# Expert weights in 4 KB rows, routing by counting beside the attention's end, and a planner with new durations: one change to a fused two-block layer kernel

## The chip, the cores and the metric

One NeuronCore of one Trainium2 chip runs the whole program. The metric is device time in microseconds (us); each kernel is timed several times, and the median counts. One further execution was taken by the hardware profiler; all rows below come from it. TensorE is called PE, its weight loads PEld, VectorE DVE, ScalarE ACT, GpSimd POOL, and SP is the engine that issues the weight loads.

## The reference, cut to what matters

256 tokens of width 1024, float32 throughout. Four parts run one after the other: an attention layer ("a"), a mixture of experts ("m"), and two hybrid layers ("0", "1").

```python
# a: two attentions over the same normed tokens, gated and added
mix = sigmoid(g_a) * out_a + sigmoid(g_b) * out_b
x = x + mix @ w_out
# m: top-1 group of 4, then top-2 of the 4 experts in it; 16 experts of width 512
t = rms_norm(x, norm_ffn_g)
g_logits = t @ w_group + b_group;  e_logits = t @ w_router + b_router
...
hid = silu(t @ w_gate[e]) * (t @ w_up[e]);  y = sum_e combine[e] * (hid @ w_down[e])
x = x + y
# 0 and 1: HGRN2 recurrence (8 heads of 128) and sliding-window attention (16 heads of 64)
y = concat(o_h, o_a) @ w_out_2;  x = x + rms_norm(y, g_post)
```

## The kernel before

**Who sets the order.** The program is written as tasks (Python generators) that yield one instruction at a time. `Sched.run` picks the next instruction of each engine when the kernel is built, from a table of durations in `Sched.op`, from priorities (`P_EDGE` first, `P_IDLE` last) and from a model of when operands are ready. What runs on the chip is a fixed list for each engine. `keep_warm` puts in dummy products (tile `warm`, on a matrix of ones, 256 columns) where the planner believes that PE would stand idle; once they are in the list they run whether PE would have waited or not. All recorded instructions carry the line of one helper (L202 before, L216 after), so rows are told apart by their tiles.

**Loads.** `plan_*` lists all weight transfers in order. `loader` issues them on SP into buffers `raw` of 1 MB, as many as `K.raw_max` allows and slots are free. Weights of parts a, 0 and 1 are split into a rounded half and a remainder (tile `w`: one ACT copy and one DVE subtraction for each 128x1024) and multiplied in three fast products; expert weights are used as they are, in full float32, so a product runs as two records. For each expert there are four units of gate and up columns (2 x 512 KB each) and two of down (1 MB each). The rows of gate and up go to partitions as `(a p)`: row 128a+p to partition p, so a partition's two pieces in one transfer are 2 KB each; a row of down is 4 KB.

**The end of part a.** `out_proj` makes the products `acc<-w,mix` (96, with 48 for the first half of the columns of `mix`, then 24 for each tile t of 128 tokens, c halves in turn). After each of the four (t, c), `Edge.tile` adds to `x`, squares it on ACT, multiplies by the gain into `hn` and has PE transpose it (`bank<-cp,hn`) into `hT`.

**Routing.** `route` multiplies `hT` with the 20 router columns (`bank<-cp,hT`, 120 columns wide, of which 20 count), then finds group, first and second expert by a chain of small DVE operations (tile `route`); `places` counts each token's place on PE; `one_hot` builds `rows`; `group(0)` gathers the tokens of four experts (`acc<-rows,x`, `bank<-rows,x`) into `xt`, and the first expert product `bank<-raw,xt` follows. In an expert: 16 products `bank<-raw,xt` (gate and up), `hidden` (ACT and DVE on `route`, then two transposes `bank<-cp,route`), 8 products `bank<-raw,route` (down, one expert behind), `acc<-rows` (back to the tokens). At expert 12 there is a branch (`overflow`, not taken here) that stands in every engine's list.

**The hybrid layers.** Projections column by column (`acc<-hh,w`, `acc<-hl,w`), the last of them `z3`; its result goes through `c_z` (ACT exp, DVE min, ACT ln, ACT exp, DVE product, all on tile `hb`) before `heads(3)` multiplies `bank<-hb,V`; then `out_proj` over `og` (192 products).

Of the kernel before, what the change touches and what calls it, by code (L numbers as in the profile page):

```python
# [20 lines left out]
BIG = 1e30  # L21
# [7 lines left out]
def _pack():  # L29
# [24 lines left out]
    parts["rank"] = np.broadcast_to(BIG * (16 - np.arange(16)[None, :]), (128, 16))  # L54
# [78 lines left out]
class Sched:  # L133
# [29 lines left out]

    def op(self, eng, op, f, a, k):
# [152 lines left out]
    def run(self):  # L317
        while self.tasks:
# [45 lines left out]
            if op == "dma_start":  # L364
                self.clk[eng] = issued = start + (1040 if eng == "POOL" else 60)
# [32 lines left out]
WIDE = 6  # L398
# [6 lines left out]
def setup(ctx, tc, I):  # L405
# [29 lines left out]
    K.gT = K.const.tile([128, 8], F32, name="gT")  # L435
    K.lev = K.const.tile([128, 10, 64], mybir.dt.uint8, name="lev")
# [61 lines left out]
def loader(K, between):  # L498
# [5 lines left out]
    def load():  # L504
        yield ("if", lambda: K.go)
        for i, u in enumerate(K.plan):
# [4 lines left out]
            for src, c in u.pieces:  # L511
                yield nc.sync.dma_start(rv[:, :, c:c + src.shape[2]], src)
# [16 lines left out]
    for i, u in enumerate(K.plan):  # L529
        yield wait(loaded[i])  # L530
        if u.how == "whole":
            u.half = raws.pop(i)
            u.flag[0].done = True
            continue
# [769 lines left out]
def plan_moe(K):  # L1304
# [19 lines left out]
def moe(K, edge, done):  # L1324
# [3 lines left out]
    K.raw_max = MOE_RAW  # L1328
# [9 lines left out]
    class Rows:  # L1338


        def __init__(self, t):
# [5 lines left out]
            self.gm, self.gs, self.e1, self.e2, self.m, self.w = (take_(1) for _ in range(6))  # L1347
            self.og, self.ge = (take_(4) for _ in range(2))
            self.L = take_(20)
            self.ee, self.o1, self.o2, self.e3, self.mask, self.first = (take_(16) for _ in range(6))  # L1350
    R = [Rows(t) for t in range(2)]
    rank = K.c("rank")

    def first_max(r, val, m, out):

        n = val.shape[1]
        yield nc.vector.tensor_reduce(m, val, axis=AX.X, op=OP.max)
        yield nc.vector.scalar_tensor_tensor(out, val, m, rank[:, 0:n], op0=OP.is_equal, op1=OP.mult)
        yield nc.vector.tensor_reduce(r.m, out, axis=AX.X, op=OP.max)

    def route(t):

        r = R[t]
        yield wait(edge.flag[t][0], K.t_router)

        pw, b_ = yield from bank(K, [128, 20 * WIDE])
        pL = pw[:, 0:20]
        sl = slice(t * 128, (t + 1) * 128)
        for k in range(8):
            yield wait(edge.flag[t][k // 4])  # L1370
            yield nc.tensor.matmul(pw, K.hh[:, k, sl], K.wide[:, 20 * k:20 * (k + WIDE)], start=(k == 0), stop=(k == 7))
# [4 lines left out]
        yield nc.vector.tensor_scalar_mul(comb[:, t, 16:17], scale, -1.0)  # L1376
        K.tinies.release(i)
        yield from first_max(r, r.L[:, 0:4], r.gm, r.og)
        g4 = lambda a: a.rearrange("p (g e) -> p g e", e=4)
        yield nc.vector.scalar_tensor_tensor(g4(r.ee), r.og[:, :, None].to_broadcast([128, 4, 4]), r.m, g4(r.L[:, 4:20]),  # L1380
                                             op0=OP.subtract, op1=OP.add)
        yield nc.vector.tensor_scalar(r.ge, r.L[:, 0:4], r.gm, None, op0=OP.subtract)
        yield from first_max(r, r.ee, r.e1, r.first)
        yield nc.vector.tensor_scalar(r.e3, r.first, r.m, -BIG, op0=OP.is_equal, op1=OP.mult)
        yield nc.vector.tensor_scalar(r.o1, r.first, r.m, None, op0=OP.is_equal)
        yield nc.vector.tensor_tensor_reduce(r.e3, r.e3, r.ee, 1.0, -3e38, OP.add, OP.max, r.e2)
        yield nc.vector.scalar_tensor_tensor(r.first, r.e3, r.e2, rank, op0=OP.is_equal, op1=OP.mult)
        yield nc.vector.tensor_reduce(r.m, r.first, axis=AX.X, op=OP.max)
        yield nc.vector.scalar_tensor_tensor(r.mask, r.first, r.m, r.o1, op0=OP.is_equal, op1=OP.add)

    def weights(t):

        r = R[t]
        yield wait(t_mask[t])
        yield nc.scalar.activation(r.ge, r.ge, AF.Exp, accum_out=r.gs)
        yield nc.vector.tensor_sub(r.e2, r.e2, r.e1)
        yield nc.scalar.activation(r.e2, r.e2, AF.Exp)
        yield nc.vector.scalar_tensor_tensor(r.w, r.e2, 1.0, r.gs, op0=OP.add, op1=OP.mult)
        yield nc.vector.reciprocal(r.w, r.w)
        yield nc.vector.tensor_sub(r.o2, r.mask, r.o1)  # L1400
        yield nc.vector.scalar_tensor_tensor(r.o1, r.o2, r.e2, r.o1, op0=OP.mult, op1=OP.add)
        yield nc.vector.tensor_scalar_mul(comb[:, t, 0:16], r.o1, r.w)
# [24 lines left out]
    t_mask = [sp(route(t), P_EDGE) for t in range(2)]  # L1427
    t_pos = [sp(places(t), P_EDGE) for t in range(2)]
# [31 lines left out]
    def halves():  # L1460
# [3 lines left out]
        for t in range(2):  # L1464
            yield from split(K, xhl[0][0][:, t], xhl[1][0][:, t], K.x[:, t])
# [5 lines left out]
    def group(q):  # L1471
# [7 lines left out]
        def part(k):  # L1479
            early = q == 0 and k < 6  # L1480
            yield wait(t_one[0] if early else t_one, t_half if q else None)
            res = K.accs if early and k < 4 else K.banks
            pg, b_ = yield from (acc_tile if res is K.accs else bank)(K, [128, 4, CAP])
# [753 lines left out]
```

## Time and profile before

| | us |
|---|---|
| three timed runs: median (lowest to highest) | 995.18 (995.14 to 996.44) |
| the profiled execution, its own time | 995.24 |
| its span, first to last instruction | 993.5 |
| PE busy | 979.1 |
| DVE busy | 691.4 |
| ACT busy | 501.2 |

The span is 1.7 us shorter than the execution's own time. The share of the span in which an engine is busy tells which engine has no room left, and dummy products count as busy. DMA moved 210.34 MB.

### The profile page before, as it was taken

What the parts mean: (1) busy time and instruction counts of PE and PEld (TensorE: products, weight loads), DVE (VectorE), ACT (ScalarE), POOL (GpSimd) and SP (SyncE); (2) the same over time, 40 slices, a digit from 0 to 9 for tenths busy, and PEclk for the clock granted to TensorE, in tenths of its full rate; (3) what the DMA queues carried; (4) which work ended last, traced back from release to release, by engine and by line L of the source; (5) the groups of instructions that cost most, each with busy time, mean ns of one, the idle gap of its engine ahead of it and who ended that gap; (6) DMA issues with size and microseconds to landing.
All of it is one profiled execution on the core that took longest, in us unless ns stands there. A gap on an engine that the chain in (4) does not pass through costs nothing.

```text
span 993.5 us, 16750 instructions
## 1 busy us (share of the span) xinstructions
PE 979.1 (99%) x6385; PEld 750.9 (76%) x6385; DVE 691.4 (70%) x1746; ACT 501.2 (50%) x1070; POOL 28.9 (3%) x67
## 2 busy tenths in 40 slices
PE   9999999999999999999999999999999999999998
PEld 8877999888434343444588989898788898988887
DVE  5778977876355434533687799899858489899952
ACT  5556879842021111110354648687755265867841
POOL 0101000000000000000000000000100000000000
PEclk9999999999999999999999999999999999999999
DMA  8822683798799999999913415432947142443331
GB/s 304 307 69 88 209 304 109 266 343 301 267 393 373 395 392 396 393 386 343 365 36 92 149 58 171 128 125 72 334 129 252 43 128 76 138 129 127 127 107 43
DMA packets 122931, 210.34 MB, mean 212 GB/s; under 512 B 6142, under 2 KB 54512, under 8 KB 122848
## 3 DMA queue, kind: packets, MB, share of 16 engines
q1 hardware_dynamic: 121632, 206.01, 59.2%
q0 software_dynamic: 1216, 3.22, 1.0%
q8 instruction: 52, 0.85, 0.4%
q14 instruction: 31, 0.25, 0.1%
HBM read 208.17 MB, written 1.05 MB: 211 GB/s over the span
## 4 chain that ended last, share of the span: by engine, by line
PE 47%; DVE 6%; DMA 1%; issue 1%; POOL 0%; ACT 0%; DVEq 0%; POOLq 0%
PE acc L202 35%; PE bank L202 11%; DVE ha L202 2%; PE warm L202 1%; DVE ap L202 1%; DMA raw<-in_w_in_dram 1%; DVE hb L202 1%; DVE w L202 1%; DVE og L202 0%; POOL sq L202 0%; DVE tiny L202 0%; DVE x L202 0%; ACT za L202 0%; DVE hn L202 0%; ACT hb L202 0%
## 5 line engine op out<-in xcount | busy, mean ns | idle before, releaser
L202 DVE TENSOR_TENSOR w<-raw,w 128x1024 fp32r<-128x1024 f32 (+1 forms) x196 | 235.3, 1220 | 28.2 <-ACT w L202 27.1
L202 PE MATMUL acc<-hh,w 128*128 128x256 f32 x1280 | 244.2, 287 | 0.0
L202 ACT ACTIVATE w<-raw 128x1024 fp32r<-128x1024 f32 (+1 forms) x196 | 198.7, 1041 | 21.9 <-PE acc L202 11.1
L202 PEld LDWEIGHTS acc<-hh,w 128*128 128x128 f32 x1280 | 201.8, 191 | 3.7 <-issue 1.4
L202 PE MATMUL acc<-hl,w 128*128 128x256 f32 x640 | 184.0, 288 | 0.0
L202 PE MATMUL acc<-w,hh 128*128 128x512 f32 (+2 forms) x512 | 155.2, 380 | 0.0
L202 PEld LDWEIGHTS acc<-hl,w 128*128 128x128 f32 x640 | 122.3, 191 | 3.5 <-issue 1.7
L202 PE MATMUL bank<-raw,xt 128*64 128x512 f32 x512 | 119.4, 600 | 0.0
L202 PEld LDWEIGHTS acc<-w,hh 128*128 128x128 f32 x512 | 92.1, 188 | 16.9 <-issue 2.1
L202 PE MATMUL acc<-w,hl 128*128 128x512 f32 (+2 forms) x256 | 96.5, 377 | 0.0
L202 ACT ACTIVATE route<-bank,route 128x256 f32<-128x256 f32 x16 | 7.6, 474 | 166.2 <-PE bank L202 166.2
L202 PE MATMUL acc<-w,og 128*128 128x512 f32 x384 | 89.1, 391 | 0.0
L202 PEld LDWEIGHTS acc<-w,og 128*128 128x128 f32 x384 | 71.7, 188 | 14.7
L202 PEld LDWEIGHTS bank<-raw,xt 128*64 128x64 f32 x512 | 33.1, 136 | 55.0 <-issue 48.7
L202 DVE TENSOR_TENSOR ha<-ha 128x256 f32<-128x256 f32 (+5 forms) x216 | 71.6, 365 | 4.2 <-PE bank L202 4.0
L202 ACT ACTIVATE ap<-ap,tiny 128x256 f32<-128x256 f32 (+1 forms) x110 | 47.8, 448 | 27.3 <-DVE tiny L202 26.8
L202 PE MATMUL bank<-raw,route 128*64 128x512 f32 x256 | 60.4, 599 | 0.0
L202 PEld LDWEIGHTS warm<-ones 128*128 128x128 f32 x325 | 45.6, 201 | 15.4 <-issue 9.1
L202 PE MATMUL warm<-ones 128*128 128x256 f32 x325 | 54.5, 309 | 2.7 <-ACT ones L424 2.4
L202 PEld LDWEIGHTS acc<-w,hl 128*128 128x128 f32 x256 | 48.3, 189 | 7.3
L202 DVE TENSOR_SCALAR route<-route 128x256 f32<-128x256 f32 (+2 forms) x24 | 6.2, 272 | 57.7 <-ACT route L202 57.6
L202 PEld LDWEIGHTS bank<-raw,route 128*64 128x64 f32 x256 | 16.8, 136 | 28.8 <-issue 25.8
(276 smaller groups left out, 1350.5 us busy)
## 6 DMA issues: line engine op xcount, KB each, us to landing
raw<-in_w_in_dram SPq DMA_DIRECT2D x68, 1024.0 KB, 6.1
raw<-in_w_gate_dram SPq DMA_DIRECT2D x64, 512.0 KB, 10.1
raw<-in_w_up_dram SPq DMA_DIRECT2D x64, 512.0 KB, 10.6
raw<-in_w_down_dram SPq DMA_DIRECT2D x32, 1024.0 KB, 11.9
raw<-in_w_out_dram SPq DMA_DIRECT2D x20, 1024.0 KB, 5.2
raw<-in_cmp_k_w_dram SPq DMA_DIRECT2D x2, 1024.0 KB, 5.8
raw<-in_cmp_v_w_dram SPq DMA_DIRECT2D x2, 1024.0 KB, 5.6
raw<-in_w_fox_up_dram SPq DMA_DIRECT2D x2, 1024.0 KB, 12.2
```

Of the source, the lines that this page charges most:

```text
L202: go = lambda: f(*a, **k)
```

## The change

- **Loads.** Gate and up rows go to partitions as `(p a)`: partition p holds rows 8p to 8p+7, so the two rows of one transfer are one run of 4 KB. `x`, `gT` and the gather read every eighth column (`k::8`) to match.
- **Routing.** The transposes take `x` itself, before the square and without the gain, which is folded into the router columns once (`gw`, one more small load on POOL). The router product is 20 columns wide. Ranks are found by comparing all pairs and counting. `moe` is started while part a still runs, so that tile 0's routing can stand among the last products of `w_out`.
- **The planner's table.** Transfers cost by run length (`_transfer`), a fast product costs 13.5 instead of 3 above its columns, an issue on SP 400 instead of 60. This moves instructions on all engines, in all parts.

```diff
         if op == "dma_start":
-            cost = int(np.prod(aps[0].shape)) * 4 / 360.0 + (1 if eng == "SP" else 20)
+            cost = self._transfer(aps)
...
-                cost = max(n * (1 if n >= 256 else 4) / 2.4, 107.0) + 3
+                cost = max(n * (1 if n >= 256 else 4) / 2.4, 107.0) + 13.5
...
-            wr = [I[nm][0, e].rearrange("(a p) c -> p a c", p=128)[:, 2 * u:2 * u + 2] for nm in ("w_gate", "w_up")]
-            K.plan.append(Unit("gu", [(wr[0], 0), (wr[1], 512)], 2, 1024, "whole"))
+            wr = [I[nm][0, e].rearrange("(p a) c -> p a c", a=8)[:, 2 * u:2 * u + 2] for nm in ("w_gate", "w_up")]
+            K.plan.append(Unit("gu", [(wr[0], 0), (wr[1], 1024)], 2, 1024, "pair"))
...
-        pw, b_ = yield from bank(K, [128, 20 * WIDE])
-        pL = pw[:, 0:20]
+        pL, b_ = yield from bank(K, [128, 20])
...
-            yield nc.tensor.matmul(pw, K.hh[:, k, sl], K.wide[:, 20 * k:20 * (k + WIDE)], start=(k == 0), stop=(k == 7))
+            yield nc.tensor.matmul(pL, K.hh[:, k, sl], K.w20[:, k], start=(k == 0), stop=(k == 7))
...
+        v = r.L.rearrange("p (g e) -> p g e", e=4)
+        yield nc.vector.tensor_tensor(r.less, v[:, :, None, :].to_broadcast([128, 5, 4, 4]),
+                                      v[:, :, :, None].to_broadcast([128, 5, 4, 4]), op=OP.is_gt)
+        for j in range(1, 4):
+            yield nc.vector.tensor_tensor(r.less[:, :, j, 0:j], v[:, :, 0:j], v[:, :, j:j + 1].to_broadcast([128, 5, j]), op=OP.is_ge)
+        yield nc.vector.tensor_reduce(r.n.rearrange("p (g e) -> p g e", e=4), r.less, axis=AX.X, op=OP.add)
...
+        yield nc.vector.tensor_scalar(r.mask, r.mask, 2.0, None, op0=OP.is_lt)
...
-        yield from first_max(r, r.L[:, 0:4], r.gm, r.og)
...
-                    yield nc.tensor.matmul(pg, K.x[:, t, c], Pm[:, t].bitcast(F32), start=(t == 0), stop=(t == 1))
+                    yield nc.tensor.matmul(pg, K.x[:, t, k::8], Pm[:, t].bitcast(F32), start=(t == 0), stop=(t == 1))
...
+                if self.nxt == "m":
+
+                    ts.append(sp(transposed(K, t, c, K.x[:, t], self.flag[t][c]), P_EDGE))
                 yield nc.scalar.activation(h, xs, AF.Square, accum_out=sm[:, c:c + 1])
                 flags[1][c].done = True
-                yield nc.vector.tensor_mul(h, xs, K.gain[:, half(c)])
...
             if part == "a":
-                yield from layer1(K, edge, new.done)
+
+                before = sp(layer1(K, edge, new.done), P_MAIN)
...
-                yield from moe(K, edge, new.done)
+                yield from moe(K, edge, new.done, before)
```

Three places on PE show what moved. In these rows `xN` counts equal instructions in a run, here one for each product. First, the end of part a: the last products of `w_out` (`acc<-w,mix`), the transposes (`cp,hn` or `cp,x`), the router (`cp,hT`), the place counts (`route,cp`, `route,ones`), the gather (`rows,x`). Before:

```order
L202 MATMUL acc<-w,mix 128x512 x71
L202 MATMUL bank<-cp,hn 128x128 x4
L202 MATMUL acc<-w,mix 128x512 x14
L202 MATMUL bank<-cp,hn 128x128 x4
L202 MATMUL acc<-w,mix 128x512 x10
L202 MATMUL bank<-cp,hn 128x128 x4
L202 MATMUL acc<-w,mix 128x512
L202 MATMUL bank<-cp,hT 128x120 x10
L202 MATMUL bank<-cp,hn 128x128 x4
L202 MATMUL bank<-cp,hT 128x120 x6
L202 MATMUL warm<-ones 128x256 x14
L202 MATMUL bank<-route,cp 128x16
```

After, from tile 0's router on:

```order
L216 MATMUL bank<-cp,hT 128x20 x8
L216 MATMUL acc<-w,mix 128x512 x10
L216 MATMUL bank<-route,ones 128x16
L216 MATMUL bank<-cp,x 128x128 x4
L216 MATMUL bank<-route,cp 128x16
L216 MATMUL acc<-w,mix 128x512 x3
L216 MATMUL bank<-cp,hT 128x20 x4
L216 MATMUL acc<-w,mix 128x512 x5
L216 MATMUL acc<-rows,x 128x256 x2
L216 MATMUL bank<-cp,x 128x128 x4
L216 MATMUL acc<-rows,x 128x256 x2
L216 MATMUL bank<-cp,hT 128x20 x4
```

Tile 0's router and place count now stand ahead of the last 18 products of `w_out`, and part of its gather ahead of tile 1's last transposes. After these rows come two gather products, 2 dummies where 29 stood, tile 1's place count, two more gather products and the first expert product.

Second, the end of the experts, from the last part of expert 15's gate and up. Before:

```order
L202 MATMUL bank<-raw,xt 64x512 x4
L202 MATMUL warm<-ones 128x256 x6
L202 MATMUL bank<-raw,xt 64x512 x4
L202 MATMUL warm<-ones 128x256 x6
L202 MATMUL bank<-raw,route 64x512 x4
L202 MATMUL bank<-cp,route 128x128 x2
L202 MATMUL warm<-ones 128x256 x4
L202 MATMUL bank<-raw,route 64x512 x4
L202 MATMUL warm<-ones 128x256 x6
L202 MATMUL bank<-raw,route 64x512 x4
```

After:

```order
L216 MATMUL bank<-raw,xt 64x512 x10
L216 MATMUL bank<-raw,route 64x512 x8
L216 MATMUL warm<-ones 128x256 x29
L216 MATMUL bank<-cp,route 128x128 x2
L216 MATMUL warm<-ones 128x256
L216 MATMUL acc<-rows 128x512
L216 MATMUL bank<-raw,route 64x512 x2
```

Before, 13 runs of dummies (65 in all) stand between the products of experts 12 to 15; after, none until one run of 29 between down of expert 14 and the transposes of expert 15. Over the whole list dummies fall from 325 to 275.

Third, the end of a hybrid layer's projections (the same in both layers), from the last product of `z3`. Before:

```order
L202 MATMUL acc<-hh,w 128x256
L202 MATMUL bank<-ha 128x128 x2
L202 MATMUL warm<-ones 128x256
L202 MATMUL bank<-cp,ap 128x128
L202 MATMUL warm<-ones 128x256
L202 MATMUL bank<-cp,ap 128x128 x2
L202 MATMUL warm<-ones 128x256 x9
L202 MATMUL bank<-cp,ap 128x128 x3
L202 MATMUL acc<-w,og 128x512 x3
```

After:

```order
L216 MATMUL acc<-hh,w 128x256
L216 MATMUL warm<-ones 128x256 x42
L216 MATMUL bank<-hb,V 128x256
L216 MATMUL bank<-hb,V 128x128
L216 MATMUL bank<-hb,V 128x256
L216 MATMUL bank<-hb,V 128x128
L216 MATMUL acc<-w,og 128x512 x7
```

The attention products that stood here before (`ha`, `cp,ap`) are now earlier, and 42 dummies in one run follow `z3`, where 11 stood.

## Rows read from the trace of the kernel before

**Rows 1.** The page, part 1: busy time of each engine.

```profile
PE 979.1 (99%) x6385; PEld 750.9 (76%) x6385; DVE 691.4 (70%) x1746; ACT 501.2 (50%) x1070; POOL 28.9 (3%) x67
```

**Rows 2.** PE by stage: window, length, busy (records), granted clock, DMA share, GB/s.

```profile
16.70:236.20 219.50, 217.81 (x1434) 1.00 0.64 219
249.50:485.80 236.30, 236.00 (x1144) 1.00 1.00 372
500.20:743.40 243.20, 241.20 (x1762) 1.00 0.40 130
```

**Rows 3.** PE in order of time, two experts: start, duration, what.

```profile
392.00 4.51 PE L202 MATMUL bank<-raw,xt 128*64 128x512 f32 x20
...
404.65 4.51 PE L202 MATMUL bank<-raw,xt 128*64 128x512 f32 x20
```

**Rows 4.** SP in order of time: down's transfers of two experts that follow each other.

```profile
380.76 2.06 SPq L202 DMA_DIRECT2D raw<-in_w_down_dram  x2
...
396.67 1.92 SPq L202 DMA_DIRECT2D raw<-in_w_down_dram  x2
```

**Rows 5.** PE in order of time, the end of part a's attention.

```profile
194.95 2.18 PE L202 MATMUL warm<-ones 128*128 128x256 f32 x17
196.97 0.27 PE L202 MATMUL bank<-cp,np 128*128 128x128 f32 x1
197.69 1.05 PE L202 MATMUL bank<-cp,np 128*128 128x128 f32 x7 [0.45 <-ACT np L202]
```

**Rows 6.** PE from the end of w_out to the first expert product.

```profile
236.06 2.39 PE L202 MATMUL bank<-cp,hT 128*128 128x120 f32 x20
...
241.26 2.31 PE L202 MATMUL warm<-ones 128*128 128x256 f32 x14
...
249.50 1.94 PE L202 MATMUL bank<-raw,xt 128*64 128x512 f32 x8
251.37 1.99 PE L202 MATMUL acc<-rows,x 128*128 128x256 f32 x8
```

**Rows 7.** DVE at tile 1's routing: its chain's first step, and the step behind it.

```profile
242.99 0.23 DVE L202 SCALAR_TENSOR_TENSOR route<-bank,tiny,b 128x20 f32<-128x20 f32 x1
...
245.98 0.17 DVE L202 SCALAR_TENSOR_TENSOR route<-bank,route 128x16 f32<-128x16 f32 x1
```

**Rows 8.** Weight loads of the gather: count, shortest, median, longest ns.

```profile
L202 PEld LDWEIGHTS acc<-rows,x x16: 186/190/192, 247.1 to 252.8; 128*128 128x128 f32 x16
```

**Rows 9.** Dummies alone in the experts' end: window, length, PE busy, PEld busy, clock, DMA.

```profile
439.50:480.70 41.20, 11.40 (x65) 8.73 (x65) 1.00 0.96 354
```

**Rows 10.** PE at expert 15's hidden values.

```profile
474.07 1.06 PE L202 MATMUL warm<-ones 128*128 128x256 f32 x6
475.06 1.94 PE L202 MATMUL bank<-raw,route 128*64 128x512 f32 x8
477.07 0.41 PE L202 MATMUL bank<-cp,route 128*128 128x128 f32 x2
```

**Rows 11.** DMA as gate and up come, then down: all engines by window; last GB/s.

```profile
366.00:371.00 5.00, 5.00 (x27) 2.46 (x27) 0.49 (x2) 0.00 (x0) 0.00 (x0) 1.00 1.06 388
372.00:377.00 5.00, 5.00 (x26) 1.55 (x24) 3.24 (x7) 1.22 (x3) 0.00 (x0) 1.00 1.03 407
```

**Rows 12.** PE in the first hybrid layer, from z3's last product to w_out.

```profile
690.68 0.28 PE L202 MATMUL acc<-hh,w 128*128 128x256 f32 x1
691.21 0.68 PE L202 MATMUL bank<-ha 128*128 128x128 f32 x4 [0.25 <-DVE tiny L202]
...
692.96 2.10 PE L202 MATMUL warm<-ones 128*128 128x256 f32 x9
...
695.19 0.95 PE L202 MATMUL acc<-w,og 128*128 128x512 f32 x3
```

**Rows 13.** ACT at the same place: a split's copies.

```profile
687.93 1.99 ACT L202 ACTIVATE w<-raw 128x1024 fp32r<-128x1024 f32 x2
```

**Rows 14.** The page, part 6: w_out's transfers, count, size, median us to landing.

```profile
raw<-in_w_out_dram SPq DMA_DIRECT2D x20, 1024.0 KB, 5.2
```

More of the change, by code (lines that the diff above doesn't have):

```diff
@@ L162, in _region, with _transfer, run @@
         return p, p + n, f * b, e * b
+    @staticmethod
+    def _transfer(aps):
+        def run(x):
+            dims, n = [d for d in x.ap if d[1] > 1], 1
+            if x.space is not None and str(x.space) != "DRAM":
+                dims = [d for d in x.ap[1:] if d[1] > 1]
+            for step, m in reversed(dims):
+                if step != n:
+                    break
+                n *= m
+            return n
+        n = min(run(x) for x in aps[:2])
+        return int(np.prod(aps[0].shape)) / n / 16 * (8 + 0.0371 * 4 * n)
     def op(self, eng, op, f, a, k):
@@ L364, in run @@
             if op == "dma_start":
-                self.clk[eng] = issued = start + (1040 if eng == "POOL" else 60)
+                self.clk[eng] = issued = start + (1040 if eng == "POOL" else 400)
                 self.dma = end = max(self.dma, issued + 1040) + cost
@@ L1321, with moe @@
 MOE_RAW, MOE_END = 19, 11
-def moe(K, edge, done):
+def moe(K, edge, done, before):
     nc, I, sch = K.nc, K.I, K.S
@@ L1327, in moe, with more_raws @@
     ident = K.c("ident")
-    K.raw_max = MOE_RAW
+    def more_raws():
+        yield wait(before)
+        K.raw_max = MOE_RAW
+    t_raws = sp(more_raws(), P_EDGE)
     tr, s_r = yield from big(K, [128, 2048], "route")
@@ L1346, in take_ @@
                 return tr[:, o[0] - n:o[0]]
[L1347 to L1350, printed above, removed]
-    R = [Rows(t) for t in range(2)]
[L1352 to L1359, printed above, removed]
+            self.gm, self.gs, self.e1, self.es, self.w = (take_(1) for _ in range(5))
+            self.ge = take_(4)
+            self.L, self.n = (take_(20) for _ in range(2))
+            self.ee, self.mask = (take_(16) for _ in range(2))
+            self.less = take_(80).rearrange("p (g i j) -> p g i j", g=5, i=4)
+    R = [Rows(t) for t in range(2)]
     def route(t):
@@ L1425, in most @@
         K.banks.release(b_)
-    t_mask = [sp(route(t), P_EDGE) for t in range(2)]
-    t_pos = [sp(places(t), P_EDGE) for t in range(2)]
+    t_mask = [sp(route(t), P_EDGE if t else P_EVAC) for t in range(2)]
+    t_pos = [sp(places(t), P_EDGE if t else P_EVAC) for t in range(2)]
     t_w = [sp(weights(t), P_EVAC) for t in range(2)]
@@ L1464, in halves @@
         for t in range(2):
[L1465 removed]
+            yield from split(K, *(a[0][:, t].rearrange("p (k d) -> p k d", k=8) for a in xhl), K.x[:, t].rearrange("p (d k) -> p k d", k=8))
     def both(a, b):
@@ L1482, in part @@
             res = K.accs if early and k < 4 else K.banks
+            if res is K.banks and q == 0:
+                yield wait(edge.flag[1])
             pg, b_ = yield from (acc_tile if res is K.accs else bank)(K, [128, 4, CAP])
@@ L1501, in group @@
         if q == 0:
+            yield ("if", lambda: len(edge.tasks) == 2)
             yield wait(t_mask, edge.tasks)
+            yield wait(t_raws)
             K.slots.release(K.s_hh, edge.room[1])
@@ L2146, in sums @@
                     return
+                if self.nxt == "m":
+                    ts.append(sp(transposed(K, t, c, K.x[:, t], self.flag[t][c]), P_EDGE))
                 yield nc.scalar.activation(h, xs, AF.Square, accum_out=sm[:, c:c + 1])
                 flags[1][c].done = True
-                yield nc.vector.tensor_mul(h, xs, K.gain[:, half(c)])
-                if self.nxt == "m":
-                    yield from transposed(K, t, c, hn, self.flag[t][c])
+                if self.nxt != "m":
+                    yield nc.vector.tensor_mul(h, xs, K.gain[:, half(c)])
             r = None
@@ L2160, in tile @@
                 yield wait(ts)
-            ts = [sp(sums(c, r), P_EDGE) for c in range(2)]
+            ts = []
+            for c in range(2):
+                ts.append(sp(sums(c, r), P_EDGE))
             if self.nxt is not None:
@@ L2190, in main @@
         edge.first()
+        before = None
         for i, part in enumerate(parts):
```

58 lines of the change are left out of this document (31 added, 27 removed).

## The prediction

> **What bounds the kernel now.** I read the busy shares first. PE is busy 979.1 of 993.5 us, and no other engine comes near it [rows 1]. Next I read PE by stage: it stands idle 1.7 us of 219.5 in the attention part, 0.3 of 236.3 in the experts and 2.0 of 243.2 in the first hybrid layer, at a granted clock of 1.00 throughout [rows 2]. The second hybrid layer runs the same list. So nothing gets shorter unless PE has less in its list, or stands less. The list holds 325 dummy products, though, and those count as busy. Seventeen of them take from 194.95 to 196.97, so one takes 2.02 / 17 = 0.12 us [rows 5].
>
> The loads look like a second bound in the experts' stage, where DMA's share is 1.00 [rows 2]. They are not one yet. Two experts that follow each other start 404.65 - 392.00 = 12.65 us apart on PE [rows 3], while down's transfers are issued 396.67 - 380.76 = 15.9 us apart [rows 4]. PE eats faster than the loads come, and lives on the buffers that were full when it began. It never ran out: expert 15's own products stand back to back with dummies between them, and I see no product that starts late. So a faster load by itself buys no time here. It buys lead.
>
> My sum is therefore an account of PE: dummies that leave the list, stalls that go or come, and the dummies and stalls that are new.
>
> **The attention part.** Before, a run of 17 dummies, 2 more and a stall of 0.45 us stand before the last attention products [rows 5]: 2.0 + 0.2 + 0.45 = 2.7 us. After, the list has none there, since the up-projection of the other attention fills the place; 14 dummies at the start become 7 (-0.8). That is -3.5 at best. A planner that places operations closer to their operands may bring small stalls back; the stage had 1.7 us of them. I take -2.5; bounds -4 and +1.
>
> **The edge and the routing.** Before, PE leaves `w_out` at 236.0 and begins the first expert product at 249.50, 13.5 us later, with a run of 14 dummies and one of 15 between [rows 6]. Tile 1's chain on DVE starts with its logits at 242.99 and takes 2.99 us [rows 7]; tile 0's chain, of the same length, ran ahead of it on DVE in that gap. After, tile 0's chain lies beside products of `w_out`. That is not free: its router and place products now stand among them. A router product took 2.39 / 10 = 0.24 us [rows 6]; twelve of them, two place counts and some 0.5 us of waiting for copies move the end of `w_out` 3.7 us later. From that end I count tile 1's path: add to x and signal 0.9, transposes 0.4, copy 0.9, four router products 0.9, logits 0.3, seven counting steps 1.7 (the seventeen small operations of the old chain took 0.18 each, from 242.99 to 245.98; dependent ones take more, and I take 0.24), place count and its two signals 0.5, place 0.2, one-hot 0.4, small operations left on DVE, gather and scaling of the first `xt` 2.4. That makes 8.6. The first expert product comes at 3.7 + 8.6 = 12.3 us instead of 13.5, which is -1.2. By then 8 instead of 4 gather products are done, at 1.99 / 4 = 0.5 us each [rows 6], another -2.0.
>
> One thing speaks against it. The gather reads every eighth column of x as its stationary operand. Its weight loads now take 190 ns [rows 8] and hide under records 0.25 us apart. No row shows a load with that step. If it doubled, 32 records would take 0.13 us more each: +4.2. If it costs nothing, 0. I take +0.5, near nothing, because the present load leaves 0.06 us of cover. [...] Together the edge gives -2.7; bounds -5 and +2.
>
> **The experts.** The steady part does not change: same products, and the loads stay ahead. I check the lead, since PE gets earlier. Gate and up came at 388 GB/s, down in 4 KB rows at 407 [rows 11]. At 407, the 4.19 MB of an expert's gate and up take 10.3 instead of 10.8 us, some 0.5 us less, 5 us over the ten experts for which the loads are the slower side. That is more than PE gains on them before the tail. If the rate did not rise, the loads would still start as much earlier as PE frees their buffers.
>
> The tail holds the largest term. Thirteen runs of dummies there are busy for 11.4 us [rows 9], less 0.09 us by which each run's last overlaps the next product: 10.2 us. After, they are gone, but one run of 29 stands between down of expert 14 and the transposes of expert 15: 29 x 0.12 = 3.5 us, whatever PE would wait. Is it shorter than the wait? Before, gate and up end at 474.07 and the transposes begin at 477.07 [rows 10], so the hidden values take 3.0 us. In the changed ACT list two weight copies stand between exp and ln, 1.0 us each [rows 13]. That makes about 5.0, and down of expert 14 covers 3.6 of it (two of the runs of rows 10). So the dummies end last. The copy of the transposed values out of PSUM stands behind two more weight copies on ACT, about 1 us. The tail gives -10.2 + 3.5 + 1.0 = -5.7; bounds -8 and -1. The next edge loses 9 dummies of 79, at most -1.1; its chain on DVE sets its end, so I take -0.5.
>
> **The hybrid layers.** Here the change costs. Before, from the end of `z3`'s last product (690.96) to the first product of `w_out` (695.19) 4.2 us pass, in which 1.1 us are real products (one `ha` product and six transposes): a hole of 3.1 [rows 12]. After, the real products stand earlier and 42 dummies fill the place: 42 x 0.12 = 5.0 us that PE must run. The work that covered the wait is used up elsewhere, so the layer pays 5.0 - 3.1 = 1.9 more. The chain behind it (ACT exp, two copies of 1.0, ln, one copy, exp, then DVE) adds to about 6.3; if that held PE, it would be 3.2. Its result is not what `hb,V` multiplies, so I take 2.3 for each layer, +4.6 for both; bounds 0 (the products moved forward fill other stalls) and +12.
>
> **The rest.** One more small load on POOL and one DVE product of 160 elements lie in the first part of a, far ahead of the routing that needs them. If they were late, tile 0's router would wait, and the products of `w_out` behind it. Splitting x with a step is off PE's path.
>
> **The sum.** -2.5 - 2.7 - 5.7 - 0.5 + 4.6 = -6.8. From the profiled execution's 995.24 that is 988.4; its time stands 0.06 above the median of the timed runs, so nothing is to be corrected. I forecast 988.5; its own range is 985 to 992.
>
> **The rivals.**
> - **Slower: the hole in the hybrid layers.** If the ln of `c_z` waits for a weight copy whose load has not landed, each layer's hole becomes 6.3 plus a load's 5.2 [rows 14], and the two layers cost 2 x (11.5 - 3.1) = 16.8 instead of 4.6: 1000.6. It decides once a hole exceeds 3.1 + 5.7 = 8.8 us. For it: the copies stand in front of ln in ACT's list, and a list cannot be changed at run time. Against: before, copies at this place ran back to back [rows 13]. Chance 0.14.
> - **The loads become the bound in the tail.** PE comes 5 us earlier and loses its dummies there; if gate and up gain no rate, experts 14 and 15 wait for their buffers and the tail's 5.7 is given back: 994. Against: 407 over 388 GB/s is in the trace [rows 11]. Chance 0.11.
> - **The strided weight loads cost in full:** +3.7 on the sum, 992. [...] Chance 0.10.
> - **The hybrid layers cost nothing,** since the planner's better durations also take out the 2.0 us of stalls in each: 988.4 - 4.6 = 984. For it: every stall that it removes is PE time. Against: 42 dummies are in the list. Chance 0.15.
>
> **How the numbers follow.** The forecast has 0.50. I widen the range to 980 and 998, which takes in 984, 992, 994 and nearly half of the slower case. What a measurement of this kernel tells from no change is about 0.2%, 2 us: faster means under 993.2, slower over 997.2. Faster: 0.50 + 0.15 + 0.07 of the strided case, and little of the loads' case, 0.73. Same: the rest of these two, 0.12. Slower: 0.15.
>
> **What would show it.** In the changed profile, PE should start the first expert product about 4 us earlier (near 246) and the last of down 10 or more us earlier (near 475). The gap after `z3` should last 5 to 6 us, filled with dummies. Gate and up should come at about 407 GB/s, with no wait of PE for them. I would be wrong if stalls of under a microsecond appear all over the hybrid layers, which the present lists, planned with too short products, happened to cover; if the clock falls where dummies left; or if the hole at expert 15 lasts much longer than its 29 dummies.

## The result, and the profile after

The changed kernel takes 1005.65 us (median of four runs, 1004.63 to 1006.59); the kernel before, beside it on the same chip, 995.81 (995.14 to 996.48). The ratio is 1.0097, with a 95% interval of 1.0082 to 1.0112. It is about 1% slower; I had forecast 988.5.

I read where the time went from the first product of each stage on PE, in the timeline of both profiles. The table gives the lengths between these firsts in us: `start` up to the first projection product, `attention` up to the first `acc<-no,w`, `edge` up to the first `bank<-raw,xt`, `experts` up to the first `acc<-w,hh` of the first hybrid layer, each hybrid layer up to the end of its last `acc<-w,og`. The other columns are kernels that are explained below (E1: 13.5 for a fast product alone; E4: transfer costs alone; E5: loads alone; E6: routing alone; E7: routing and transfer costs).

| | before | after | E1 | E4 | E5 | E6 | E7 |
|---|---|---|---|---|---|---|---|
| start | 16.7 | 17.7 | 16.6 | 16.1 | 16.6 | 16.9 | 17.3 |
| attention | 184.6 | 186.0 | 184.7 | 184.5 | 184.8 | 185.4 | 185.8 |
| edge | 48.2 | 46.6 | 48.0 | 48.2 | 48.6 | 46.5 | 46.5 |
| experts | 250.7 | 249.8 | 252.1 | 246.1 | 255.2 | 252.8 | 246.3 |
| first hybrid layer | 243.2 | 248.3 | 248.2 | 243.1 | 243.1 | 243.2 | 243.0 |
| second hybrid layer | 243.3 | 248.3 | 248.2 | 243.2 | 243.3 | 243.2 | 243.3 |

After against before: start +1.0, attention +1.4, edge -1.6, experts -0.9, hybrid layers +5.0 each. That is the +9.9 between the two spans.

The page's busy line of the changed kernel, which answers to [rows 1], and PE by stage, which answers to [rows 2] (window, length, busy, granted clock, DMA share, GB/s):

```profile
PE 975.9 (97%) x6335; PEld 748.5 (75%) x6335; DVE 701.4 (70%) x1755; ACT 496.7 (50%) x1054; POOL 23.2 (2%) x64
```

```profile
17.70:242.26 224.56, 220.98 (x1434) 0.99 0.63 217
250.31:486.26 235.95, 228.02 (x1100) 0.99 0.99 382
500.15:748.41 248.26, 246.06 (x1792) 1.00 0.35 118
```

PE is still the bound, but it now stands idle 7.9 us among the experts where it stood 0.3, and the clock is no longer at 1.00 throughout. In the hybrid layer it is busy 5 us longer with the same products and 31 more dummies.

The first 44.0 us of the first hybrid layer, up to the first `acc<-hh,w`, are as long after as before. The rest in two parts, the projections up to the end of `z3`'s last product and what stands behind it, before and after:

```profile
544.19:690.96 146.77, 145.75 (x1289) 1.00 0.37 116
690.96:743.42 52.46, 51.82 (x240) 1.00 0.66 231
```

```profile
544.14:696.90 152.76, 151.06 (x1309) 1.00 0.31 97
696.90:748.41 51.51, 51.40 (x253) 1.00 0.67 235
```

The part with the 42 dummies got 0.95 us shorter; the projections ahead of them got 6.0 longer. Products that moved ahead of `z3` (`ha` 0.44, `cp,ap` 0.69, `ap,kv` 1.24, by their time on PE before) are 2.4 us of that. For the other 3.6 PE in order of time shows shorter runs. The score products of two heads, before and then after:

```profile
672.65 0.93 PE L202 MATMUL bank<-kv,qaT 64*128 64x128 f32 x8
```

```profile
673.99 0.92 PE L216 MATMUL bank<-kv,qaT 64*128 64x128 f32 x4
...
675.63 0.92 PE L216 MATMUL bank<-kv,qaT 64*128 64x128 f32 x4
```

Eight records in one run take as long as four (0.93 and 0.92 us): two heads' products, each on 64 rows, run beside each other when they are neighbours in the list (their records start in pairs, 0.01 us apart). After, they stand apart, and the second head costs 0.85 us more. In the list before one pair of heads stands apart too. Over the layer PE is busy 9.0 us with score products before and 9.9 after, waits left out.

PE behind `z3`, which answers to [rows 12]:

```profile
696.62 0.28 PE L216 MATMUL acc<-hh,w 128*128 128x256 f32 x1
696.75 3.50 PE L216 MATMUL warm<-ones 128*128 128x256 f32 x28
699.72 2.20 PE L216 MATMUL warm<-ones 128*128 128x256 f32 x17
701.76 1.47 PE L216 MATMUL bank<-hb,V 128*128 128x256 f32 x8
702.99 1.87 PE L216 MATMUL acc<-w,og 128*128 128x512 f32 x7
```

(Three of the dummies stand in both rows, where two windows meet.) The tail of the experts on all engines but PEld, which answers to [rows 10]:

```profile
467.66 3.60 PE L216 MATMUL bank<-raw,route 128*64 128x512 f32 x16
...
470.54 2.36 DVE L216 TENSOR_TENSOR w<-raw,w 128x1024 fp32r<-128x1024 f32 x2 [0.19 <-ACT w L216]
...
471.19 3.74 PE L216 MATMUL warm<-ones 128*128 128x256 f32 x29
471.36 0.46 ACT L216 ACTIVATE route<-bank,route 128x256 f32<-128x256 f32 x1
472.16 2.01 ACT L216 ACTIVATE w<-raw 128x1024 fp32r<-128x1024 f32 x2 [0.34 <-DMA raw<-in_w_in_dram]
472.82 0.29 DVE L216 TENSOR_SCALAR route<-route 128x256 f32<-128x256 f32 x1
473.25 2.36 DVE L216 TENSOR_TENSOR w<-raw,w 128x1024 fp32r<-128x1024 f32 x2
474.07 0.85 ACT L216 ACTIVATE route<-route 128x256 f32<-128x256 f32 x2
...
475.97 2.36 DVE L216 TENSOR_TENSOR w<-raw,w 128x1024 fp32r<-128x1024 f32 x2
...
478.24 0.48 DVE L216 SCALAR_TENSOR_TENSOR route<-bank,route 128x256 f32<-128x256 f32 x1
...
478.87 0.41 PE L216 MATMUL bank<-cp,route 128*128 128x128 f32 x2 [3.94 <-DVE route L216]
```

Between the steps of expert 15's hidden values stand splits of the next layer's weights, copies on ACT and subtractions of 2.36 us a pair on DVE. The 29 dummies end at 474.9; PE waits on to 478.87.

PE's windows of 2 us around two of its longest waits, columns as above:

```profile
110.00:112.00 2.00, 0.53 (x3) 0.84 1.11 365
112.00:114.00 2.00, 2.00 (x11) 0.50 1.04 344
114.00:116.00 2.00, 2.00 (x17) 0.80 0.19 64
480.00:482.00 2.00, 2.00 (x6) 0.50 1.06 369
482.00:484.00 2.00, 2.00 (x7) 0.64 1.10 351
```

Behind the wait of 3.94 us, and behind one of 2.30 us for DVE's `tq` at 111.47, PE runs for some 3.4 us at a granted clock of 0.50 (an estimate from these windows). In the first dip a fast product of 256 columns takes 0.21 to 0.22 us (from 114.07 to 114.28 and from 112.57 to 112.79 on PE), against 0.12 at a clock of 1.00. So I count a window of 2 us at clock c as a loss of 2 x (1 - c), and estimate the first dip at 0.3 + 1.0 + 0.4 and the second at 1.0 + 0.7: 1.7 us each.

### The profile page after: what moved, and what is told of

It reads as the page before. It is cut to its first block, busy times and chain, and to the rows that moved or that the text cites. A ratio compares the mean times of both kernels' runs of the same rounds, so it can differ in the third digit from the quotient of the medians.

```text
span 1003.4 us, 16635 instructions
## 1 busy us (share of the span) xinstructions
PE 975.9 (97%) x6335; PEld 748.5 (75%) x6335; DVE 701.4 (70%) x1755; ACT 496.7 (50%) x1054; POOL 23.2 (2%) x64
## 3 DMA queue, kind: packets, MB, share of 16 engines
HBM read 208.16 MB, written 1.05 MB: 208 GB/s over the span
## 4 chain that ended last, share of the span: by engine, by line
PE 46%; DVE 8%; ACT 1%; issue 1%; DVEq 0%
PE acc L216 32%; PE bank L216 12%; DVE ha L216 3%; DVE w L216 2%; PE warm L216 1%; DVE ap L216 1%; ACT ha L216 1%; DVE hb L216 1%; DVE hn L216 0%; DVE rows L216 0%; DVE tiny L216 0%; DVE x L216 0%; DVE og L216 0%; DVE za L216 0%; ACT w L216 0%
## 5 line engine op out<-in xcount | busy, mean ns | idle before, releaser
L216 PE MATMUL acc<-hh,w 128*128 128x256 f32 x1280 | 247.4, 289 | 0.0
L216 PE MATMUL acc<-hl,w 128*128 128x256 f32 x640 | 184.8, 289 | 0.0
L216 PEld LDWEIGHTS acc<-w,hh 128*128 128x128 f32 x512 | 92.6, 188 | 17.3 <-issue 2.2
L216 DVE TENSOR_TENSOR ha<-ha 128x128 f32<-128x128 f32 (+5 forms) x216 | 69.3, 352 | 0.6
L216 ACT ACTIVATE ap<-ap,tiny 128x256 f32<-128x256 f32 (+1 forms) x98 | 42.9, 448 | 49.0 <-DVE tiny L216 36.5
L216 PE MATMUL warm<-ones 128*128 128x256 f32 x275 | 40.1, 297 | 4.6 <-ACT ones L437 2.4
L216 PEld LDWEIGHTS warm<-ones 128*128 128x128 f32 x275 | 36.3, 198 | 8.1 <-ACT ones L437 2.4
L216 PE MATMUL bank<-ha 128*64 128x96 f32 (+2 forms) x608 | 37.9, 246 | 0.0
```

The lines of the kernel that those rows point to most:

```text
L216: go = lambda: f(*a, **k)
```

## The experiments

Theory A: the loss lies in the planner's one entry for a fast product, which rearranges the hybrid layers. Theory B: it comes from the routing begun early and the new layout, and the table only shifts dummies. Medians are given against the kernel before in the same session.

**E1. The entry of 13.5 alone, in the kernel before.**

```diff
-                cost = max(n * (1 if n >= 256 else 4) / 2.4, 107.0) + 3
+                cost = max(n * (1 if n >= 256 else 4) / 2.4, 107.0) + 13.5
```

> The kernel before, with one entry of the planner's table changed: a fast product costs 13.5 above its columns instead of 3. Old loads, old routing. Theory A (this entry rearranges the hybrid layers and the attention, and that is where the loss lies): each hybrid layer about 248.3 instead of 243.2 us, the attention part up to the first product of w_out about 2 us longer, experts as before: 1006 to 1009. Theory B (the loss comes from the routing begun early and the new layout of the loads, the table only shifts dummies): 994 to 997.

1007.28 against 996.57, ratio 1.0114 (1.0097 to 1.0131): +10.7. The projections of its first hybrid layer:

```profile
545.52:698.19 152.67, 151.00 (x1309) 1.00 0.35 111
```

The whole loss of the hybrid layers is there, with old loads and old routing. The attention part did not get longer, which theory A had wrong.

**E2. The changed kernel with that entry back at 3.**

```diff
-                cost = max(n * (1 if n >= 256 else 4) / 2.4, 107.0) + 13.5
+                cost = max(n * (1 if n >= 256 else 4) / 2.4, 107.0) + 3
```

> The changed kernel with that one entry set back to 3; everything else as changed. Theory A: the hybrid layers come back to 243.2 us each (-10) and the attention part loses most of its 2.4 us: 993 to 996. Theory B: the loss stays, 1003 to 1006.

991.71 against 996.57, ratio 0.9943 (0.9921 to 0.9964), below theory A's range. The projections take 146.74 us again:

```profile
541.19:687.93 146.74, 145.74 (x1289) 1.00 0.32 101
```

So theory A holds for the hybrid layers from both sides, and the rest of the change is a gain.

**E3. The changed kernel with the whole old table:** E2's edit, and

```diff
-            cost = self._transfer(aps)
+            cost = int(np.prod(aps[0].shape)) * 4 / 360.0 + (1 if eng == "SP" else 20)
...
-                self.clk[eng] = issued = start + (1040 if eng == "POOL" else 400)
+                self.clk[eng] = issued = start + (1040 if eng == "POOL" else 60)
```

> The changed kernel (4 KB loads, counting, early routing) with the whole old table of durations. Theory A: what remains is the edge's gain of 1.6 us and a gain of up to 1 us among the experts, so 993 to 995.5. Theory B: 1002 or more.

1000.37, ratio 1.0051 (1.0035 to 1.0067): between the two theories, in neither's range. The hybrid layers are as before, the edge is 1.7 us shorter, but the experts take 254.3 us. Loads and routing carry a loss of their own; E5 and E6 split it.

**E4. The transfer costs alone, in the kernel before** (with the method `_transfer` put in).

```diff
...
-            cost = int(np.prod(aps[0].shape)) * 4 / 360.0 + (1 if eng == "SP" else 20)
+            cost = self._transfer(aps)
```

> The kernel before with only the planner's cost of a transfer changed. In its list the 65 dummies among experts 12 to 15 become 6, and the hybrid layers keep their old list but for a few places. If dummies in the tail cost PE their own time, as the prediction had it: 10 us less, 986 to 988. If they mostly lay in waits that PE has anyway (theory A, from the changed kernel's tail, which gained 0.4 us for 50 dummies less): 993 to 997.

991.80, ratio 0.9961 (0.9946 to 0.9975): -4.8, between the two expectations. The 65 dummies of the tail become 6, and of the 10 us half comes back as waits, 1.99 us at the branch and 1.81 at expert 15 (below) the largest.

```profile
472.03 3.23 PE L217 MATMUL bank<-raw,route 128*64 128x512 f32 x14 [1.81 <-ACT route L217]
```

**E5. The loads alone,** with the step of eight that they need; PE's list is that of before, row for row.

```diff
-            K.plan.append(Unit("gu", [(wr[0], 0), (wr[1], 512)], 2, 1024, "whole"))
+            K.plan.append(Unit("gu", [(wr[0], 0), (wr[1], 1024)], 2, 1024, "pair"))
...
-                    yield nc.tensor.matmul(pg, K.x[:, t, c], Pm[:, t].bitcast(F32), start=(t == 0), stop=(t == 1))
+                    yield nc.tensor.matmul(pg, K.x[:, t, k::8], Pm[:, t].bitcast(F32), start=(t == 0), stop=(t == 1))
...
```

> The kernel before with only the 4 KB rows of gate and up (with the columns of x taken at a step of eight to match); the order on PE is that of before, row for row. The prediction's reading: +0.5 for the gather, the split of x hidden, the faster loads buy nothing: 995.5 to 997. Theory A, from the changed trace, where a weight load of the gather takes 337 instead of 190 ns, a split of x 2.0 instead of 1.2 us, and PE waits 1.5 us for a DVE step behind it: +1.8, +1.5 to +1.9 and +0.6, so 999.5 to 1001.

999.88 against 995.44, ratio 1.0049 (1.0032 to 1.0066): +4.4, as theory A had it. Four views follow: the weight loads of the gather, which answer to [rows 8], and the splits of x in the changed kernel; the splits of x before; PE behind them in E5; and PE's clock there.

```profile
L216 PEld LDWEIGHTS acc<-rows,x x16: 312/337/338, 241.9 to 252.9; 128*128 128x128 f32 x16
...
L216 DVE TENSOR_TENSOR xl<-x,xh x2: 1992/2060/2129, 291.6 to 293.7; 128x1024 fp32r<-128x1024 f32 x2
...
L216 ACT ACTIVATE xh<-x x2: 2070/2126/2181, 289.1 to 291.1; 128x1024 fp32r<-128x1024 f32 x2
```

```profile
L202 DVE TENSOR_TENSOR xl<-x,xh x2: 1218/1222/1226, 291.4 to 292.5; 128x1024 fp32r<-128x1024 f32 x2
...
L202 ACT ACTIVATE xh<-x x2: 1041/1049/1057, 289.8 to 290.7; 128x1024 fp32r<-128x1024 f32 x2
```

```profile
297.76 0.33 PE L202 MATMUL bank<-cp,route 128*128 128x128 f32 x1 [1.93 <-DVE route L202]
```

```profile
300.00:302.00 2.00, 2.00 (x6) 0.50 0.92 276
302.00:304.00 2.00, 2.00 (x11) 0.67 0.64 262
```

A weight load takes 337 instead of 190 ns, a split 2.13 us instead of 1.05 on ACT and 2.06 instead of 1.22 on DVE. The copies that the next transposes need stand behind the splits on DVE, PE waits 1.93 us, and then runs at a granted clock of 0.50 to 0.67 from 300 to 304 us, which costs 1.7 more in this execution (by its windows, as above). The +4.4 does not hang on that dip: two of the four runs kept a mean clock of 1.000 and took 999.47 and 999.60.

**E6. The routing alone:** the changed kernel with E3's edit and E5's undone.

```diff
-                    yield nc.tensor.matmul(pg, K.x[:, t, k::8], Pm[:, t].bitcast(F32), start=(t == 0), stop=(t == 1))
+                    yield nc.tensor.matmul(pg, K.x[:, t, c], Pm[:, t].bitcast(F32), start=(t == 0), stop=(t == 1))
...
```

> The kernel before with only the new routing; same list on PE as the changed kernel with the old table. If the new layout is what costs among the experts there, this one has the edge's gain of 1.7 us and no loss behind it: 994 to 996. If the routing itself is the loss (its operations on DVE stand in the way of the first experts), 998 to 1001. A third case: with 2 instead of 29 dummies at the edge the granted clock falls there in some executions, which would add 1 to 3 us and scatter.

997.52, ratio 1.0020 (1.0010 to 1.0029): +2.1. The edge is 1.7 us shorter; the experts take 2.1 more. That is between the first two cases. The third shows: PE waits 0.82 us for `xt` and the clock falls:

```profile
250.00:252.00 2.00, 2.00 (x6) 0.50 0.95 353
252.00:254.00 2.00, 2.00 (x10) 0.89 0.41 65
```

Beside that, and in none of the cases, PE waits 2.01 us behind the branch at expert 12, where it waited 0.16.

**E7. Routing and transfer costs, without the new loads, 13.5 and 400:** E6 with

```diff
-            cost = int(np.prod(aps[0].shape)) * 4 / 360.0 + (1 if eng == "SP" else 20)
+            cost = self._transfer(aps)
```

> The kernel before with the new routing and, of the table, only the cost of a transfer; old layout of the loads, old costs of a product and of an issue. By the single runs: 4.8 for the transfer and 1.7 for the edge, so 988.5 to 991.5, and below the changed kernel by 15. If the two gains are the same waits, 991 to 993.

988.91 against 995.44, ratio 0.9925 (0.9908 to 0.9943): 6.5 us faster than before, and 16.7 below the changed kernel. In its four runs the mean granted clock was 0.993 to 1.000, and those at 1.000 took 986.44 and 988.01; the profiled one, which the table shows, is the one at 0.993.

**E8. The changed kernel without the two runs of 42 dummies.**

```diff
-            go()
+            if not 600e3 < until < 940e3:
+                go()
```

> The changed kernel without the two runs of 42 dummies behind z3; otherwise the same list. The prediction's reading (the chain of c_z is about as long as the dummies): the time stays within 2 us, 1003.5 to 1006.5, or is longer where the clock falls in the hole. If the dummies themselves hold PE, since the product behind them does not need the chain: up to 5.0 us less for each layer, 996 to 1000.

1006.73 (1006.08 to 1012.98). PE in the first hybrid layer behind `z3`:

```profile
695.60 1.47 PE L216 MATMUL bank<-hb,V 128*128 128x256 f32 x8
696.83 1.87 PE L216 MATMUL acc<-w,og 128*128 128x512 f32 x7
702.42 0.79 PE L216 MATMUL bank<-sq,ones 128*128 128x512 f32 x1 [3.72 <-ACT sq L216]
```

The dummies did hold the eight products `hb,V`, which need no chain; without them PE waits 3.72 us a little later, and the clock falls (a mean of 0.992 in this execution, 0.996 in the changed kernel's). So the hole is real, and the dummies are not what makes the layer 5 us longer. They are not free either: the part behind `z3` takes 52.8 us here against 51.5, but 2.6 us of it go to the clock, so at full clock it would be some 1.3 us shorter than with them (an estimate from these rows).

**E9. E7 with 120 router columns again.**

```diff
-            yield nc.tensor.matmul(pL, K.hh[:, k, sl], K.w20[:, k], start=(k == 0), stop=(k == 7))
+            yield nc.tensor.matmul(pw, K.hh[:, k, sl], K.wide[:, 20 * k:20 * (k + 6)], start=(k == 0), stop=(k == 7))
...
```

> The routing and transfer kernel (988.9) with the router's products at 120 columns again, of which 20 count; nothing else. There the granted clock is at 1.2 GHz for about 4 us behind the edge (246 to 252 us), in some executions. If the narrow router products are what lets it fall, the clock at the edge stays at 1.00 and the median goes to 986.5 to 988. If the missing dummies or the waits let it fall, the same dip shows and the time is 988.5 to 991.

989.30, ratio 0.9935 (0.9918 to 0.9952), with the same dip at 246 to 250 us (0.64 and 0.51 in its two windows of 2 us). The 1.2 GHz of the expectation is a granted clock of 0.50, at which 256 columns took 0.21 us above: 1.2 columns in a ns. The narrow router is not its cause.

**E10. The issue cost alone, in the kernel before.**

```diff
-                self.clk[eng] = issued = start + (1040 if eng == "POOL" else 60)
+                self.clk[eng] = issued = start + (1040 if eng == "POOL" else 400)
```

> The kernel before with only the planner's cost of an issue on SP changed, 60 to 400. Theory A: the hybrid layers keep their list, nothing among the experts changes but a few places, so 994 to 997. A rival: later planned loads put waits among the splits of the attention part, 998 to 1001.

996.61 against 996.02, ratio 1.0005 (0.9996 to 1.0015): nothing.

**E11. The kernel before without 12 of its first 47 dummies; E13. E7 with 48 more of them.** Both lists are else unchanged. E11, then E13:

```diff
-            go()
+            if not 4700 < until < 5600:
+                go()
```

```diff
+        if not K.more:
+            K.more = True
+            for _ in range(48):
+                o = K.nc.tensor.matmul(ps, K.one_r, K.one_r[:, None, :].to_broadcast([128, 2, 128]), start=True, stop=True)
...
+                o.alts[0][3]()
```

> The kernel before without 12 of the 47 dummies at its start, which only shifts the place of everything behind them in PE's program. PE's wait behind the branch at expert 12 is 0.16 us before and 1.75 to 2.01 us in the changed kernel and the experiments that change PE's list. If that wait depends on where the branch stands in the program, it may become some 1.8 us here with an unchanged list around it; if it comes of what stands around the branch, it stays at 0.16. The time itself within 2 us of before, unless the clock falls at the start.

> The routing and transfer kernel with 48 more dummies at its very start, nothing else. By my count of PE's instructions this puts the branch at expert 12 where it stands in the three kernels that waited 0.16 us there (5422 to 5430 instructions from the start; 5424 here, 5328 without). If the place in the program sets that wait, it falls from 1.95 to about 0.2 us, and the dip of the clock behind it goes. If what stands around the branch sets it, it stays near 1.95. The 48 dummies cost up to 5.8 us at the start, less what PE waits there anyway, so the time itself comes to 988 to 992.

PE's first product behind the branch, before, in E11 and in E13:

```profile
430.27 0.41 PE L202 MATMUL bank<-cp,route 128*128 128x128 f32 x2 [0.16 <-PEq L1636]
```

```profile
432.91 0.41 PE L202 MATMUL bank<-cp,route 128*128 128x128 f32 x2 [1.97 <-PEq L1637]
```

```profile
430.88 0.41 PE L216 MATMUL bank<-cp,route 128*128 128x128 f32 x2 [0.16 <-PEq L1660]
```

Moving the branch in the program makes the wait and takes it away. E11 took 999.52 (one run), with a dip of the clock behind the wait (0.50 at 434 to 436 us). E13 took 993.28, above the 988 to 992 expected: its start got 3.9 us longer, and while no dip follows the branch, one stands at 474 to 478 us (0.62 and 0.52 in its two windows of 2 us).

**E12. The changed kernel with 8 in place of 13.5.**

```diff
-                cost = max(n * (1 if n >= 256 else 4) / 2.4, 107.0) + 13.5
+                cost = max(n * (1 if n >= 256 else 4) / 2.4, 107.0) + 8
```

> The changed kernel with a fast product at 8 instead of 13.5 above its columns. In its list the hybrid layers have 17 dummies behind z3 (42 at 13.5, 11 at 3), more changes between fast and full products, and 17 runs of ap,kv. If the loss grows with the entry, a hybrid layer takes 245 to 246.5 us; if it depends on how each list happens to fall, anything from 243 to 249; if the accurate value alone were at fault, 243.2.

996.76 (one run). A hybrid layer takes 244.0 us: 0.8 more than at 3, 4.3 less than at 13.5. It falls outside the first case, below its 245, and leaves the second: it depends on how each list happens to fall.

**E14, E15. Both heads' score products from one task, in the changed kernel and in E7.**

```diff
+            for a, b, k in ((0, 128, 0), (128, 384, 128)):
+                for j in range(2):
...
+                    yield nc.tensor.matmul(bk[j][0][:, a:b], qaT[r, c, i % 4, k:k + 128], kk, start=True, stop=True)
```

> The changed kernel with the score products of both heads of a pair (kv,qaT: rows 0 to 63 and 64 to 127) issued by one task, one head's behind the other's, in place of two tasks which the planner separates. Theory A (the lost neighbourhood of such products is a large part of the 3.6 us by which the projections of a hybrid layer got longer): eight runs of eight at 0.9 us in place of 9.9 us in all, so 2 to 2.5 us less for each layer, 1000 to 1002.5. Rival (the planner's changed places and the waits on DVE make up the 3.6 us): within 1.5 us of the changed kernel, 1004 to 1007.

999.19 against 995.94, ratio 1.0042 (1.0029 to 1.0054), below theory A's range. A hybrid layer takes 245.7 us instead of 248.3. PE is busy 8.1 us with score products there (9.9 in the changed kernel, 9.0 before), waits left out. But 1.7 us of waits for DVE now stand inside their runs, where the changed kernel has none; with them the products take 9.8 us, against 9.9 in the changed kernel. The 2.6 us are therefore a gain of the whole list that the planner made around the pairs, in which `ap,kv` for instance took 0.8 us less in the projections. What neighbours alone are worth is not isolated.

> The same pairing in the routing and transfer kernel (988.9). By the same price (9.1 us of score products for each layer become some 7.2): 985 to 987, if the list around them stays as good; its dummies behind z3 change from 11 to 17. If the planner's list falls worse around the pairs, 989 to 993.

991.87, ratio 0.9958 (0.9941 to 0.9974): 3 us worse than E7. The projections got 2.4 us shorter (144.4 against 146.7), but the part behind `z3` 3.6 longer (56.1 against 52.5): six transposes, eight `ha` and eight `ap,kv` stand there now that stood ahead, with 1.7 us of waits and 17 dummies instead of 11. Where a list's small products stand decides as much as how they pair.

## Why the prediction was wrong

**Three terms failed by about 5 us or more each.** On the table's boundaries I had forecast -2.5 for the start and the attention, and measured was +2.4; -1.2 for the edge, and it was -1.6; -7.7 for the experts (what the edge's term gains in their stage, the tail and the next edge), and it was -0.9; +4.6 for the two hybrid layers, and it was +10.0.

**The parts alone do not simply add up.** They measured +10.7 (13.5), -4.8 (transfer), +0.6 (issue), +4.4 (loads) and +2.1 (routing), together +13.0. The branch's wait of some 1.8 us is in three of them; counted once, +9.4 are left, and +9.8 was measured. That agreement is partly luck. The same sum gives +0.5 for E2 (all but the 13.5), and -4.9 was measured; -4.5 for E7, and it was -6.5; +6.5 for E3, and it was +3.8. In the changed kernel the entry costs 14.7 us, not 10.7. So what one part costs depends on which of the others are in.

**The hybrid layers: the step that failed, and the one that turns a gain into a loss** (E1 has the loss alone; without it, E2, the change is a gain). I took +2.3 for each layer; it was +5.0. The hole itself was right in its mechanism: 42 dummies, 5.0 us; E8 shows the wait behind them. Once the 2.4 us of products that moved ahead are added back, the part behind `z3` costs 1.4 us more than before. What I put at nothing, without a reason, is what else the list does when the entry moves every product: the projections got 3.6 us longer beyond the products that moved. My sentence on what would make me wrong named stalls there; idle time rose by only 0.7 us. The larger part is time in which PE counts as busy: 0.9 us more for score products, whose neighbours on half the rows are torn apart, and some 2.1 us in amounts of up to 0.6 over the other kinds of product. That shorter runs of small products are the cause of these 2.1 is argued and not shown; I can't pin them to single rows.

**The experts' tail: mis-sized.** I forecast -5.7 there and -0.5 for the next edge; the whole stage got only 0.9 us shorter. The dummies went, as said. But the hole at expert 15 is 7.7 us (471.2 to 478.87), not 4.5: I counted the copies on ACT in its chain and left out the subtractions on DVE, of which the rows show three pairs between its steps. The clock fell behind that wait (1.7), the branch cost 1.6 more, and the wait behind the split of x 1.5. E4, without the new loads, the new routing and the 13.5, keeps a gain of 4.8 in spite of the branch's wait.

**Loads.** That the faster load buys nothing was right: the transfers came at 406 and 411 GB/s in the windows of [rows 11] that had 388 and 407, and no product among the experts waited for one.

```profile
366.00:371.00 5.00, 5.00 (x26) 2.40 (x26) 1.59 (x5) 0.00 (x0) 0.00 (x0) 1.00 1.03 406
372.00:377.00 5.00, 5.00 (x26) 1.62 (x24) 2.22 (x5) 1.69 (x4) 0.00 (x0) 1.00 1.03 411
```

The step of eight was sized within its bounds on PE: by E5's profile the gather's 32 products took 1.2 us more (I took 0.5, bounds 0 and 4.2), against 4.7 us by which their 32 weight loads got longer (147 ns each), so these hid in part. The sentence "splitting x with a step is off PE's path" was wrong: that cost 1.9 us and a dip of the clock. With the step a weight load took 147 ns more and a split 0.8 to 1.1 us more; the doubled weight load behind the rival's +3.7 was my estimate, and 337 ns is 1.8 times 190.

**The edge was right in its mechanism.** `w_out` ends 3.6 us later from its start (3.7 forecast), and the first expert product comes 8.2 us behind it (8.6 forecast):

```profile
250.31 1.94 PE L216 MATMUL bank<-raw,xt 128*64 128x512 f32 x8 [0.62 <-DVE xt L216]
```

But the clock falls behind the edge in E6 (0.50 at 250 to 252 us) and in E7 (246 to 252 us), where 2 dummies are left of 29. E2 and E3 have the same 2, and mean clocks of 0.995 and 0.997 in their profiles; the changed kernel has them too, and its profile shows 1.00 from 244 to 256 us. Of the times that I had named as signs two did not come: the first expert product starts at 250.3 us, not near 246, and the last of down ends at 486.3, not near 475.

**The attention part** was to gain 2.5 us and lost 2.4, start included. The dummies went; a wait of 1.94 us at 17.48 came, one at 111.47 grew to 2.30 from 0.95, and the clock took 1.7. E1 has the second wait and no dip (a mean clock of 1.000), and no loss in this part. No single part of the change has this loss (E1 +0.1, E4 -0.7, E5 +0.1, E6 +1.0), nor has E2 (+0.6); E7 has +1.8, in an execution with a mean clock of 0.993. Beyond these waits its cause stays open.

## What to carry to other kernels

An entry of a planner's table is one change to every list that it makes: try each entry alone, and read the new list for what leaves a wait uncovered and which small products lose their neighbours, since that cost appears as busy time. A more accurate number gave the worse list here: a fast product of 256 columns takes 0.12 us in the rows, and the planner has 0.1205 with the entry of 13.5 and 0.110 with 3, yet 13.5 cost 10.7 us, and 8 cost 0.8 in a hybrid layer. When the layout of a tile changes, cost every reader of it on every engine, and what is queued behind that reader.

## What the hardware showed that I had not expected

The same branch, by which PE jumps over the code for the overflow, cost it 0.16 us or 1.75 to 2.01, by its place in the program alone (E11, E13). By my count the kernels at 5422 to 5430 PE instructions have the short wait, and all eleven others that I counted, at 5286 to 5398, the long one. What in the place sets the wait, no run here shows.

Waits of some 2 to 4 us on PE with no dummies in them were in several places followed by some 3.4 us at a granted clock of 0.50 (behind 3.94 and 2.30 us in the changed kernel, 1.93 in E5 and 1.97 in E11; not in E1, behind 2.34 us, nor in the changed kernel behind its waits of 1.94 and 1.79), and then cost 1.7 us more than their own length, by the windows of 2 us. In E6 a dip follows a wait of only 0.82, so these runs give no length from which on a wait is dear. Before, with 325 dummies, the mean clock was 0.997 to 1.000 in all runs; in the changed kernel 0.993 to 0.996.
